# Token factors of an MLP as a row through DRAM, and the order of loads and PSUM banks in its lower stage

## The chip, the cores and the metric

The kernel runs on one core of one Trainium2 chip. The metric is device microseconds of one execution; less is better. One profiled execution comes with instruction times of all engines.

## The reference, cut to what matters

One decoder layer over 1032 tokens (1024 of a prompt and 8 of a sample batch) with 1024 channels: a mixer of attention and retention, a cross-attention into memory tokens, and an MLP, each behind an RMSNorm and with a residual addition. The change lies in the MLP:

```python
def rmsnorm(x, g):
    xf = x.astype(jnp.float32)
    y = xf * lax.rsqrt(jnp.mean(xf * xf, axis=-1, keepdims=True) + EPS)
    return (y * g.astype(jnp.float32)).astype(x.dtype)

def sq_relu_mlp(h, w_up, w_down):
    return jnp.square(jax.nn.relu(h @ w_up)) @ w_down

xp = xp + sq_relu_mlp(rmsnorm(xp, norm_mlp[l]), w_up[l], w_down[l])
```

All is float32. The hidden width is 4096.

## The kernel before, in words

Channels lie on partitions, tokens in columns. A float32 operand is split into a high part (`wh`, `UH`, `T_h`) by an ACT cast and a low part (`wl`, `UL`, `T_l`) by a DVE subtraction, and a product of two operands takes three matmuls: high by high, high by low, low by high. Tokens are handled in four column groups of 258 (`QC`): two halves of 516 tokens by two chunks, `c` = 0 and 1. `QCOLS[2 * c + half]` are the columns.

*Before the MLP* the output projection of the cross-attention runs over `(ft, c)`, channel tile by column group, in a list `order` written out by hand; here `c` runs over the four column groups, and the list ends with (6, 2), (7, 2), (4, 3), (5, 3), (6, 3), (7, 3). Each step evicts its bank by a DVE addition into `xs` (L1716); ACT scales it by the MLP's gain (L1719) and squares it (L1724); POOL adds the squares into `ssum` (L1725); ACT's DMA queue stores `xs` to `X3` in DRAM (L1726).

*Token factors.* `norm_factor(x)` makes the RMSNorm's factor of column group `x`: a matmul with a 128x128 tile of ones sums `ssum` over partitions and repeats the sum on all of them, ACT takes the square root (L1612), DVE the reciprocal (L1613), and the factors stay in `ssum`. They are applied after the upper projection, in `hidden`: DVE computes max(product, 0) times the factor (L1772) and ACT squares it (L1773).

*The upper stage* does the projection to the hidden width with seven products instead of eight in each 2x2 block (a Strassen-Winograd form). There are 16 blocks `b`; `up_block` runs products `q` in the order 1, 6, 2, 7, 5, 4, 3, and inside each the chunks. A product is twelve matmuls of 258 columns (L1747). Banks are called X (q 1 and 2), Z (6, 7 and 4) and Y (5 and 3), two of each; two more banks hold other tiles, the sums of `norm_factor` among them. `p1` is an ACT copy of X (L1794), `u2` and `u3` are Z plus `p1` (L1797, L1802), the quadrants 22, 21, 12 are formed at L1806. When all four quadrants of a chunk are there, ACT's queue stores three of them to `HQ`, and POOL forms four differences `ht` (L1779 to L1782) and stores them to `HT` (L1783). Block 0 runs for chunk 0 alone first, while the operands of chunk 1 are being made (`first_half`, `second_half`), then for chunk 1.

*The lower stage* goes back to 1024 channels, also with seven products, over four groups `g` of hidden rows and, inside each, four pairs `p` of output tiles. For each group, `raw_d` tiles hold the weights of the pairs; `left_lower` casts and splits them into `wd` (L1875, L1876), for product 6 after differences on DVE and POOL (L1885 to L1889). `right_lower` loads hidden operands from `HQ` or `HT` into `raw_h` on SP (L1862) and splits them (L1868, L1869). Products run in stages (1, 2), (6,), (7, 4), (5, 3); stages of two products run pairs 0 and 1 first, then 2 and 3; stage (6,) runs all four pairs. Each product is again twelve matmuls (`dn`, L1897), and its bank is added by DVE into result tiles `C` (L1977), or copied by ACT (L1975) for product 1 of the first group. `residual_rows` loads the residual from `X3` into `C` on SP (L1849). At the end, `finish` makes the final norm's factors with Sqrt and reciprocal and stores.

*What sets the order.* TensorE's instructions in both stages keep the order of the program (`tc.keep_in_program_order`). The instructions of the other engines and of the DMA queues are put in order by the framework's planner, which goes by its own modelled times; each engine and each queue then runs its list strictly in that order. `tc.issue_after(ins)` puts what follows behind `ins` on its queue. A tile waits, when its memory was used before, for the last user of that tile (`reuse_waits="tile"`). In the first group the weights of pair 0 are issued by SP and those of pairs 1 to 3 by POOL:

```python
(nc.gpsimd if g == 0 and p else nc.sync).dma_start(raws[p][x][:, :1024], i["wall"][U_DN + 8 * g + 2 * p + x])
```

The eight lower banks come from one pool tag with eight buffers (`tag="acc", bufs=8`). The first tiles of pairs 2 and 3 (`raw_d0_2_0`, `raw_d0_3_0`) lie in the memory of the last block's `hq` tiles, of chunk 0 and chunk 1.

An existing function, `rstd_bcast` (L1150 to L1165), makes the factors of an earlier norm in another way: sums in one row, an ACT copy (L1159), a DMA that lays the row out as 86 partitions by 12 columns (L1161), multiply-add on DVE and power -0.5 on POOL (`rsqrt_small`, L120 and L121), a DMA to DRAM (L1164) and one that reads the row back to all 128 partitions (L1165).

Of the kernel before, what the change touches and what calls it, by code (L numbers as in the profile page):

```python
# [10 lines left out]
F32 = mybir.dt.float32  # L11
# [8 lines left out]
P = 128  # L20
D = 1024
# [27 lines left out]
def decoder_step(ctx: ExitStack, tc: tile.TileContext, i: dict, o: dict):  # L49
# [1515 lines left out]
    for q, kt, half in ((1, 0, lo_h), (6, 0, hi_h), (2, 4, lo_h), (3, 4, hi_h)):  # L1565
        for c in range(2):
            cq = slice(half.start + c * QC, half.start + c * QC + QC)
            RIGHT[q, c] = [x[:, kt : kt + 4, cq] for x in (UH, UL)]
# [38 lines left out]
    def norm_factor(x):  # L1607
        cs = QCOLS[x]
        fp = PD.tile([P, 512], F32, tag=("mk", "dt")[x % 2], name=f"rm_{x}", bufs=1)[:, :QC]
        mm(fp, onesq, ssum[:, cs], True, True)  # L1610
        rf = ssum[:, cs]
        nc.scalar.activation(rf, fp, AF.Sqrt, scale=1.0 / D, bias=epsc)  # L1612
        nc.vector.reciprocal(rf, rf)  # L1613
# [26 lines left out]
    with pool("e") as A, pool("e_ps", space=PSUM) as PS:  # L1640
# [59 lines left out]
        for n, (ft, c) in enumerate(order):  # L1700
# [36 lines left out]
            if (ft, c) == (5, 3):  # L1737
                parts_st.close()
                right_tiles(1, 5, 7)

# [11 lines left out]

    def up_block(b, W, chunks):

# [9 lines left out]
        def hidden(quad, src, c):  # L1764
            if c not in HQ_:
                if (b, c) == (0, 0):
                    HQ_[c] = N.tile([P, 4, QC], F32, tag="hq0", name="hq_0_0")
                else:
                    HQ_[c] = N.tile([P, 4, QC], F32, tag=f"xq{2 + c}_0", name=f"hq_{b}_{c}")
            h = HQ_[c]  # L1770
            r = small("r", f"{quad}_{c}", 4) if quad == 11 else src
            nc.vector.scalar_tensor_tensor(r, src, 0.0, ssum[:, QCOLS[2 * c + HALF_OF[quad]]], ALU.max, ALU.mult)  # L1772
            nc.scalar.activation(h[:, PLACE[quad], :], r, AF.Square)  # L1773
            if quad == 12:
                nc.scalar.dma_start(HQ[b, c].rearrange("p (x j) -> p x j", x=3), h[:, 0:3, :])

                h11, h21, h22, h12 = (h[:, x, :] for x in range(4))
                t = N.tile([P, 4, QC], F32, tag=f"xq{2 + c}_1", name=f"ht_{b}_{c}")
                nc.gpsimd.tensor_sub(t[:, 0, :], h12, h11)  # L1779
                nc.gpsimd.tensor_sub(t[:, 1, :], h22, t[:, 0, :])  # L1780
                nc.gpsimd.tensor_sub(t[:, 2, :], h22, h12)
                nc.gpsimd.tensor_sub(t[:, 3, :], h21, t[:, 1, :])  # L1782
                nc.gpsimd.dma_start(HT[b, c].rearrange("p (x j) -> p x j", x=4), t)  # L1783

        for q in (1, 6, 2, 7, 5, 4, 3):
            for c in chunks:
# [11 lines left out]
                elif q == 2:  # L1798
                    hidden(11, ps, c)
                elif q == 7:  # L1800
                    u3[c] = small("u3", c)
                    nc.vector.tensor_add(u3[c], ps, p1[c])  # L1802
                else:
                    quad, x = {5: (22, u3), 4: (21, p1), 3: (12, u2)}[q]
                    r = small("r", f"{quad}_{c}", 4)
                    nc.vector.tensor_add(r, ps, x[c])  # L1806
                    hidden(quad, r, c)
# [7 lines left out]
    norm_factor(0)  # L1815
    norm_factor(1)
    with pool("h") as HP, pool("s_ps2", space=PSUM) as SP:
        pin[0] = True
        up_block(0, w0, (0,))
# [4 lines left out]
        norm_factor(2)  # L1824
        norm_factor(3)
# [11 lines left out]
    STAGES = [(1, 2), (6,), (7, 4), (5, 3)]  # L1837
    SOURCE = {1: (HQ, 0), 2: (HQ, 1), 3: (HQ, 2), 5: (HT, 0), 6: (HT, 1), 7: (HT, 2), 4: (HT, 3)}
    taken = [0, 0]
    with pool("acc", side="right") as AC, pool("w") as A, pool("w_ps", space=PSUM) as PS:  # L1840

# [5 lines left out]
        def residual_rows(quad):  # L1847
            kh, hs = {11: (0, lo_h), 21: (4, lo_h), 22: (4, hi_h), 12: (0, hi_h)}[quad]
            nc.sync.dma_start(C[quad], X3[kh : kh + 4, :, hs].rearrange("k p c -> p k c"))  # L1849
# [64 lines left out]
        def finish(c, half):  # L1914
            tail = tails[c] if half else None
            cs = QCOLS[2 * c + half]
            fp = PS.tile([P, 512], F32, tag="acc", name=f"fin_{c}_{half}", bufs=8)[:, :QC]
# [15 lines left out]
        for g in range(4):  # L1933
# [10 lines left out]
            for p, x in ((0, 0), (0, 1), (1, 0), (1, 1), (2, 0), (2, 1), (3, 0), (3, 1)):  # L1944

                (nc.gpsimd if g == 0 and p else nc.sync).dma_start(raws[p][x][:, :1024], i["wall"][U_DN + 8 * g + 2 * p + x])
            for stage in STAGES:
                if (g, stage[0]) == (0, 1):
                    residual_rows(11)
                S = {q: right_lower(g, q) for q in stage}  # L1950
                if (g, stage[0]) == (0, 7):

                    with tc.issue_after(seen["SP"]):
                        for quad in (22, 21, 12):
                            residual_rows(quad)
                end = g == 3 and stage == (5, 3)
                batches = [(0, 1), (2, 3)] if len(stage) == 2 else [(0, 1, 2, 3)]
                if end:
                    batches = [(0, 1, 2, 3)]
                bank = {}  # L1960
                steps = [(q, p, c) for batch in batches for q in stage for p in batch for c in range(2)]
                if end:
                    steps = [(q, p, c) for c in range(2) for q in stage for p in range(4)]
                W = {}
                for n, (q, p, c) in enumerate(steps):
                    if (q, p) not in W:
                        W[q, p] = left_lower(g, p, q)
                    if q == stage[0]:
                        bank[p, c] = PS.tile([P, 512], F32, tag="acc", name=f"dn_{g}_{q}_{p}_{c}", bufs=8)[:, :QC]
                    ps = bank[p, c]  # L1970
                    lower(W[q, p], S[q], c, ps, q == stage[0])
# [212 lines left out]
```

## Time and profile before

| what | value |
|---|---|
| median of three runs | 1566.5 us |
| the three runs | 1566.5, 1566.89, 1562.6 us |
| profiled execution, its time | 1562.22 us |
| its span, first to last instruction | 1560.5 us |
| mean granted TensorE clock | 0.988 |
| PE busy | 1497.6 us (96%) |
| DVE, ACT, POOL busy | 1070.7, 651.0, 442.5 us |
| DMA | 230.02 MB, mean 147 GB/s |

Times in the views are microseconds from the span's start. PE is TensorE's matmuls, PEld its weight loads, DVE VectorE, ACT ScalarE, POOL GpSimd, SP SyncE; a `q` behind an engine's name (SPq) is its DMA-issuing queue. In the timeline a row has start, duration, engine, line, operation, out<-in, and in brackets the engine's idle time before it and what ended it; consecutive instructions of one kind are merged into one row with a count, and their durations overlap. In the waits a row has who waited for whom, then the total in us, the number of times and the longest. A fenced row starts where the profile puts it; releasers are inferred from semaphores. The upper stage starts near 873 us, the lower stage at 1209.8 us.

### The profile page before, as it was taken

What the parts mean: (1) busy time and instruction counts of PE and PEld (TensorE: products, weight loads), DVE (VectorE), ACT (ScalarE), POOL (GpSimd) and SP (SyncE); (2) the same over time, 40 slices, a digit from 0 to 9 for tenths busy, and PEclk for the clock granted to TensorE, in tenths of its full rate; (3) what the DMA queues carried; (4) which work ended last, traced back from release to release, by engine and by line L of the source; (5) the groups of instructions that cost most, each with busy time, mean ns of one, the idle gap of its engine ahead of it and who ended that gap; (6) DMA issues with size and microseconds to landing.
All of it is one profiled execution on the core that took longest, in us unless ns stands there. A gap on an engine that the chain in (4) does not pass through costs nothing.

```text
span 1560.5 us, 26766 instructions
## 1 busy us (share of the span) xinstructions
PE 1497.6 (96%) x10483; PEld 1395.5 (89%) x10483; DVE 1070.7 (69%) x2096; ACT 651.0 (42%) x1265; POOL 442.5 (28%) x457
## 2 busy tenths in 40 slices
PE   9989999999899899999999899999999899999997
PEld 7667868999859789989899899999999799999996
DVE  4224422898875744566686988888788588787887
ACT  6314332665652332036634543333334343334454
POOL 0343311113452520134322233433334402020360
PEclk9999999999999999999999999999999899999998
DMA  8635343313675246462584244434335872636313
GB/s 286 173 92 166 82 112 95 88 38 96 176 272 196 77 163 179 147 188 99 153 275 148 91 147 150 150 136 150 136 137 182 275 231 80 196 85 201 97 42 109
DMA packets 121875, 230.02 MB, mean 147 GB/s; under 512 B 14210, under 2 KB 74481, under 8 KB 121621
## 3 DMA queue, kind: packets, MB, share of 16 engines
q1 hardware_dynamic: 91508, 170.30, 34.9%
q0 software_dynamic: 21024, 41.10, 8.6%
q10 hardware_dynamic: 9216, 16.91, 2.8%
q8 instruction: 82, 1.34, 0.4%
q14 instruction: 45, 0.36, 0.1%
HBM read 168.93 MB, written 57.52 MB: 145 GB/s over the span
## 4 chain that ended last, share of the span: by engine, by line
PE 48%; DVE 12%; DMA 5%; issue 4%; ACT 3%; POOL 1%; DVEq 0%; POOLq 0%; ACTq 0%; SPq 0%
PE dn L1897 17%; PE Z L1747 7%; PE mq L67 5%; PE Y L1747 5%; PE pr_m L67 4%; PE X L1747 4%; PE pr_o L67 3%; DVE wu L1586 1%; DMA raw_up<-in_wall 1%; DVE dacc L1187 1%; PE mpv L67 1%; PE ms L67 1%; DMA raw_d<-in_wall 1%; POOL ck L546 1%; DVE wd L1876 1%
## 5 line engine op out<-in xcount | busy, mean ns | idle before, releaser
L1897 PE MATMUL dn<-UH,wd 128*128 128x258 f32 x1792 | 328.7, 285 | 7.6 <-ACT wd L1875 4.4
L1897 PEld LDWEIGHTS dn<-UH,wd 128*128 128x128 f32 x1792 | 280.4, 191 | 9.3 <-ACT wd L1875 4.9
L1897 PE MATMUL dn<-UL,wd 128*128 128x258 f32 x896 | 254.6, 284 | 0.0
L1897 PEld LDWEIGHTS dn<-UL,wd 128*128 128x128 f32 x896 | 170.9, 191 | 0.1
L1773 ACT ACTIVATE hq<-r 128x258 f32<-128x258 f32 x128 | 53.6, 419 | 161.1 <-DVE r L1772 160.9
L1977 DVE TENSOR_TENSOR c<-c,dn 128x258 f32<-128x258 f32 x216 | 88.2, 417 | 36.9 <-PE dn L1897 34.8
L1747 PE MATMUL Z<-T_h,wu 128*128 128x258 f32 x512 | 100.1, 287 | 6.4 <-DVE u L1797 4.7
L1875 ACT CAST wd<-raw_d 128x512 fp32r<-128x512 f32 x96 | 58.9, 618 | 104.8 <-PE dn L1897 84.7
L1586 DVE TENSOR_TENSOR wu<-raw_up,wu 128x512 fp32r<-128x512 f32 x96 | 91.9, 958 | 9.1 <-ACT wu L1585 9.1
L1747 PE MATMUL X<-UH,wu 128*128 128x258 f32 x512 | 97.7, 283 | 0.4 <-ACT p L1794 0.4
L110 DVE TENSOR_TENSOR wl_u<-raw_u,wh_u 128x1024 fp32r<-128x1024 f32 x46 | 58.4, 1279 | 57.3 <-ACT wh_u L109 55.4
L1747 PEld LDWEIGHTS Z<-T_h,wu 128*128 128x128 f32 x512 | 81.4, 189 | 9.5 <-DVE u L1797 7.1
L1876 DVE TENSOR_TENSOR wd<-raw_d,wd 128x512 fp32r<-128x512 f32 x96 | 75.4, 789 | 18.0 <-ACT wd L1875 17.9
L1747 PEld LDWEIGHTS X<-UH,wu 128*128 128x128 f32 x512 | 81.3, 188 | 0.7 <-ACT p L1794 0.6
L109 ACT CAST wh_u<-raw_u 128x1024 fp32r<-128x1024 f32 x50 | 52.2, 1050 | 70.9 <-PE mq L67 43.6
L1868 ACT CAST UH<-raw_h 128x1032 fp32r<-128x1032 f32 x56 | 58.8, 1055 | 51.6 <-PE dn L1897 30.9
L1779 POOL TENSOR_TENSOR ht<-hq 128x258 f32<-128x258 f32 x32 | 23.4, 730 | 200.8 <-ACT hq L1773 186.8
L1869 DVE TENSOR_TENSOR UL<-raw_h,UH 128x1032 fp32r<-128x1032 f32 x56 | 76.3, 1362 | 5.3 <-ACT UH L1868 5.3
L1889 POOL TENSOR_TENSOR raw_d<-raw_d,raw_d 128x512 f32<-128x512 f32 x16 | 23.4, 1460 | 182.0 <-DVE raw_d L1885 127.6
L1747 PE MATMUL Z<-T_l,wu 128*128 128x258 f32 x256 | 72.4, 283 | 0.0
L1747 PE MATMUL X<-UL,wu 128*128 128x258 f32 x256 | 72.2, 282 | 0.0
L1585 ACT CAST wu<-raw_up 128x512 fp32r<-128x512 f32 x96 | 57.1, 610 | 30.6 <-DVE raw_up L1592 23.7
(483 smaller groups left out, 4630.8 us busy)
## 6 DMA issues: line engine op xcount, KB each, us to landing
raw_u<-in_wall SPq DMA_DIRECT2D x59, 512.0 KB, 4.6
HT<-ht POOLq DMA_DIRECT2D x32, 516.0 KB, 3.0
raw_h<-HT SPq DMA_DIRECT2D x32, 516.0 KB, 4.4
raw_up<-in_wall SPq DMA_DIRECT2D x32, 512.0 KB, 3.6
raw_d<-in_wall SPq DMA_DIRECT2D x26, 512.0 KB, 4.5
HQ<-hq ACTq DMA_DIRECT2D x32, 387.0 KB
raw_h<-HQ SPq DMA_DIRECT2D x24, 516.0 KB, 4.5
cmk<-in_cmk SPq DMA_DIRECT2D x16, 512.0 KB, 4.8
```

Source lines behind the costliest of these rows:

```text
L67: pinned(nc.tensor.matmul(out, l, r, start=start, stop=stop))
L110: (lo_engine or nc.vector).tensor_sub(wl[:, :n], raw[:, :n], wh[:, :n].bitcast(F32))
L1585: nc.scalar.copy(w[:, :512], src)
L1586: nc.vector.tensor_sub(w[:, 512:], src, w[:, :512].bitcast(F32))
L1747: pinned(nc.tensor.matmul(ps, l, r[:, k, :], start=first and k == 0 and x == 0, stop=k == 3 and x == 2, skip_group_check=True))
L1773: nc.scalar.activation(h[:, PLACE[quad], :], r, AF.Square)
L1868: nc.scalar.copy(h, rv)
L1869: nc.vector.tensor_sub(l, rv, h.bitcast(F32))
L1875: nc.scalar.copy(w[:, :512], src)
L1876: nc.vector.tensor_sub(w[:, 512:], src, w[:, :512].bitcast(F32))
L1897: pinned(nc.tensor.matmul(ps, l, r[:, k, cq], start=first and k == 0 and x == 0, stop=k == 3 and x == 2, skip_group_check=True))
L1977: nc.vector.tensor_add(y, y, ps)
```

## The change

- `norm_factor` goes. `norm_rows(c, row_tile)` makes the factors of the two column groups of one chunk: two matmuls against a single column of ones, an ACT copy of each one-partition row, a DMA on ACT's queue into `col` (86 partitions, three columns for each group), multiply-add and power -0.5 on POOL, POOL's DMA to DRAM and two POOL DMAs that read the rows back to all partitions, into `ssum`. It is called for chunk 0 after the projection step (7, 2), and for chunk 1 inside block 0's first run, behind product 2 and ahead of its `hidden`.
- In block 15, chunk 1, the four `ht` differences go from POOL to DVE.
- In the lower stage's first group all weights are issued by SP: pairs 0 and 1 first, pairs 2 and 3 after the operand loads of products 1, 2 and 6; the residual of quadrant 11 is loaded in two halves around product 6's operands; operands of 7 and 4, then the other residuals, are put behind these loads. Its products run as (1, 2) on pairs 0 and 1, 6 on pairs 0 and 1, (1, 2) on pairs 2 and 3, 6 on pairs 2 and 3. The other groups keep their order.
- The eight lower banks get tags `acc0` to `acc7`, placed in this order and taken in turn.

```diff
+    def norm_rows(c, row_tile):
+        for x in (2 * c, 2 * c + 1):
+            cx = slice(3 * x, 3 * x + 3)
+            rp = PD.tile([P, 512], F32, tag=("mk", "dt")[x % 2], name=f"rm_{x}", bufs=1)[:1, :QC]
+            mm(rp, ones, ssum[:, QCOLS[x]], True, True)
+            row = row_tile(x)[:1]
+            nc.scalar.copy(row, rp)
+            nc.scalar.dma_start(col[:, cx], row)
+        cc = slice(6 * c, 6 * c + 6)
+        nc.gpsimd.tensor_scalar(col[:, cc], col[:, cc], 1.0 / D, EPS, ALU.mult, ALU.add)
+        nc.gpsimd.tensor_tensor(col[:, cc], col[:, cc], half[:86, 0:1].to_broadcast([86, 6]), op=ALU.pow)
+        r = rrow[3:4, 2 * c * QC : (2 * c + 2) * QC]
+        nc.gpsimd.dma_start(r.rearrange("a (x p k) -> p (a x) k", x=2, k=3), col[:, cc].rearrange("p (x k) -> p x k", x=2))
+        for x in range(2):
+            nc.gpsimd.dma_start(ssum[:, QCOLS[2 * c + x]], bcast_rows(r[:, x * QC : x * QC + QC], P, QC))
...
+            if (ft, c) == (7, 2):
+                norm_rows(0, lambda x: A.tile([P, QC], F32, tag="xs", name=f"nrow_{x}", bufs=3))
...
+                eng = nc.vector if (b, c) == (15, 1) else nc.gpsimd
...
                 elif q == 2:
+                    if then:
+                        then()
                     hidden(11, ps, c)
...
-    norm_factor(0)
-    norm_factor(1)
...
-        up_block(0, w0, (0,))
+        up_block(0, w0, (0,), lambda: norm_rows(1, lambda x: HP.tile([P, QC], F32, tag="r", name=f"nrow_{x}", bufs=4)))
...
-        norm_factor(2)
-        norm_factor(3)
...
+        turns = [0]
+        for x in BANK_ORDER:
+            PS.tile([P, 512], F32, tag=f"acc{x}", name=f"acc{x}_order", bufs=1)
+        def acc_bank(name):
+            turns[0] += 1
+            return PS.tile([P, 512], F32, tag=f"acc{(turns[0] - 1) % 8}", name=name, bufs=1)[:, :QC]
...
-            for p, x in ((0, 0), (0, 1), (1, 0), (1, 1), (2, 0), (2, 1), (3, 0), (3, 1)):
-                (nc.gpsimd if g == 0 and p else nc.sync).dma_start(raws[p][x][:, :1024], i["wall"][U_DN + 8 * g + 2 * p + x])
+            load_left((0, 1) if g == 0 else range(4))
+            parts = [((1, 2), (1, 2), (0, 1)), ((), (1, 2), (2, 3)), ((6,), (6,), (0, 1)), ((), (6,), (2, 3))]
+            if g == 0:
+                parts = [parts[0], parts[2], parts[1], parts[3]]
+            parts += [((7, 4), (7, 4), (0, 1)), ((), (7, 4), (2, 3)), ((5, 3), (5, 3), (0, 1)), ((), (5, 3), (2, 3))]
+            if g == 3:
+                parts[-2:] = [((5, 3), (5, 3), (0, 1, 2, 3))]
+            for new, qs, ps_ in parts:
+                if g == 0 and 7 in new:
+                    with tc.issue_after(seen["SP"]):
+                        S.update({q: right_lower(g, q) for q in new})
                     with tc.issue_after(seen["SP"]):
                         for quad in (22, 21, 12):
                             residual_rows(quad)
+                else:
+                    S.update({q: right_lower(g, q) for q in new})
+                if g == 0 and 1 in new:
+                    residual_rows(11, (slice(0, 2),))
+                if g == 0 and 6 in new:
+                    residual_rows(11, (slice(2, 4),))
+                    load_left((2, 3))
```

More of the change, by code (lines that the diff above doesn't have):

```diff
@@ L1605, in put @@
         nc.vector.tensor_sub(l, src, h.bitcast(F32))
[L1607 to L1613, printed above, removed]
+    col = KC.tile([86, 12], F32, tag="ncol", name="ncol")
+    def norm_rows(c, row_tile):
[13 more added lines that the diff above has]
+            nc.gpsimd.dma_start(ssum[:, QCOLS[2 * c + x]], bcast_rows(r[:, x * QC : x * QC + QC], P, QC))
     def first_half(c):
@@ L1916, in finish @@
             cs = QCOLS[2 * c + half]
-            fp = PS.tile([P, 512], F32, tag="acc", name=f"fin_{c}_{half}", bufs=8)[:, :QC]
+            fp = acc_bank(f"fin_{c}_{half}")
             mm(fp, onesq, ssf[:, cs], True, tail is None)
@@ L1955, in decoder_step @@
                             residual_rows(quad)
-                end = g == 3 and stage == (5, 3)
-                batches = [(0, 1), (2, 3)] if len(stage) == 2 else [(0, 1, 2, 3)]
-                if end:
[L1959 to L1964, printed above, removed]
+                else:
[5 more added lines that the diff above has]
+                    load_left((2, 3))
+                end = g == 3 and 5 in qs
+                steps = [(q, p, c) for q in qs for p in ps_ for c in range(2)]
+                if end:
+                    steps = [(q, p, c) for c in range(2) for q in qs for p in ps_]
                 for n, (q, p, c) in enumerate(steps):
@@ L1967, in decoder_step @@
                         W[q, p] = left_lower(g, p, q)
-                    if q == stage[0]:
-                        bank[p, c] = PS.tile([P, 512], F32, tag="acc", name=f"dn_{g}_{q}_{p}_{c}", bufs=8)[:, :QC]
+                    if q == qs[0]:
+                        bank[p, c] = acc_bank(f"dn_{g}_{q}_{p}_{c}")
                     ps = bank[p, c]
-                    lower(W[q, p], S[q], c, ps, q == stage[0])
+                    lower(W[q, p], S[q], c, ps, q == qs[0])
                     cq = slice(c * QC, c * QC + QC)
```

32 lines of the change are left out of this document (17 added, 15 removed).

## The prediction

> **What bounds the kernel now.** I read the page's busy times first, then the windows of TensorE, then the waits and the timeline at the two places that the change touches.
>
> ```profile
> PE 1497.6 (96%) x10483; PEld 1395.5 (89%) x10483; DVE 1070.7 (69%) x2096; ACT 651.0 (42%) x1265; POOL 442.5 (28%) x457
> ```
>
> TensorE is the bound: it is busy for 1497.6 of 1560.5 us, and the change takes no product away. Time can only come from what TensorE loses between products: gaps, and stretches at a lower clock. The windows show where it loses (stretch, its length, PE busy, matmuls, granted clock, DMA share, GB/s):
>
> ```profile
> core 0: us, PE busy (x), PEclk, DMA share, GB/s
> 872.80:892.40 19.60, 17.18 (x131) 1.00 0.38 115
> 892.40:895.00 2.60, 0.69 (x6) 1.00 0.51 199
> 1209.80:1250.00 40.20, 33.22 (x233) 0.87 0.79 268
> 1300.00:1400.00 100.00, 100.00 (x838) 1.00 0.47 138
> 1214.60:1218.00 3.40, 3.40 (x19) 0.51 0.71 239
> 1229.50:1235.40 5.90, 5.78 (x25) 0.52 1.03 412
> ```
>
> Undisturbed, 838 matmuls take 100 us: 0.119 us each, 1.43 us for a product of twelve. In the first 40.2 us of the lower stage stand 233 matmuls, worth 233 x 0.1193 = 27.8 us. So 12.4 us are lost there: 40.2 - 33.2 = 7.0 us idle, and 5.4 us in the two stretches at half clock. The waits of 860 to 910 us (first three rows, the start of the upper stage) and of 1195 to 1260 us (the start of the lower stage) name what ended the gaps:
>
> ```profile
> PE Z L1747 <- DVE u L1797: 2.8, 2, 1.9
> PE Z L1747 <- DVE xs L1716: 1.1, 1, 1.1
> PE X L1747 <- ACT p L1794: 0.4, 1, 0.4
> ...
> PE dn L1897 <- ACT wd L1875: 4.4, 1, 4.4
> PE dn L1897 <- DVE r L1806: 1.8, 1, 1.8
> PE dn L1897 <- DVE wd L1876: 0.6, 1, 0.6
> ```
>
> That is 4.3 us at the first place and 6.8 us at the second. Everything the change can win lies here, some 17 us with the slow clock.
>
> **Part 1: the token factors.** Out go four Sqrt on ACT, four reciprocals on DVE and the Sqrt table's load at this place. The timeline around them:
>
> ```profile
> 875.41 1.28 ACT L1612 ACT_TABLE_LOAD   x1
> ...
> 877.45 3.37 DVE L1613 RECIPROCAL ssum<-ssum 128x258 f32<-128x258 f32 x2
> ...
> 878.15 0.37 ACT L1794 COPY p<-X 128x258 f32<-128x258 f32 x1
> ...
> 880.75 0.35 DVE L1797 TENSOR_TENSOR u<-Z,p 128x258 f32<-128x258 f32 x1
> ...
> 887.07 1.03 PE L67 MATMUL rm<-ssum,onesq 128*128 128x258 f32 x4
> ...
> 892.23 1.75 DVE L1613 RECIPROCAL ssum<-ssum 128x258 f32<-128x258 f32 x1
> ```
>
> The copy `p`, for which TensorE waited 0.4 us, stands behind the table load and two Sqrt. The first `u`, released at 880.75, stands behind two reciprocals that end at 880.8; the second, longest wait (1.9 us) stands behind the reciprocal of 892.23. With them gone 0.4 + 2.8 = 3.2 us go. The 1.1 us for `xs` stay: the bank is released by a DVE addition that is queued behind operand splits, not behind factors. The sums over partitions remain four matmul groups at the same 258 columns, only earlier on the queue: 0.
>
> What comes in is a chain: sum, ACT row copy, ACT's DMA into `col`, two POOL operations, POOL's DMA to DRAM, POOL's DMA that reads the row back to all partitions. The kernel does the same for its second norm, once for the whole row, on the SP queue:
>
> ```profile
> 578.94 0.72 SPq L1161 DMA_DIRECT2D rcol<-rrow  x1
> 581.00 0.17 DVE L120 TENSOR_SCALAR rcol<-rcol 86x12 f32<-86x12 f32 x1 [2.12 <-DMA rcol<-rrow]
> 581.25 2.27 POOL L121 TENSOR_TENSOR rrc<-rcol,half 86x12 f32<-86x12 f32 x1 [6.63 <-DVE rcol L120]
> 583.55 0.25 SPq L1164 DMA_DIRECT2D rrow<-rrc  x1
> 585.23 0.33 SPq L1165 DMA_DIRECT2D rb<-rrow  x1
> ...
> 588.83 0.94 DVE L1329 SCALAR_TENSOR_TENSOR qm<-mq,rb 128x344 f32<-128x344 f32 x2 [7.66 <-DMA rb<-rrow]
> ...
> L121 POOL TENSOR_TENSOR rm<-sm,half x1: 708/708/708, 599.8 to 599.8; 128x2 f32<-128x2 f32 x1
> ...
> HT<-ht POOLq DMA_DIRECT2D x32, 516.0 KB, 3.0
> ```
>
> From these rows: DMA into the column 2.1 us (578.94 to 581.00), power between 0.7 us (2 columns) and 2.3 us (12 columns), so 1.3 us for 6, the write 1.7 us (583.55 to 585.23), or 3.0 us if it goes like POOL's own stores, the read back 3.6 us (585.23 to 588.83). With 0.8 us for two row copies and at most 0.7 us for the POOL multiply-add, a chain takes 10.2 to 11.5 us. In a sentence by itself: the Trainium skill, page "DMA: Bandwidth & Descriptors", section "Anatomy of one DMA", gives each DMA issued by POOL about 2.0 us of fixed time, nearly all of it the receipt of the write, by which three in a row would be an estimated 6 to 7 us; the rows' 7.4 us are what I use.
>
> Is that hidden? The first pair's chain starts after the product (7,2), four projection products (24 matmuls, 2.86 us each) before the upper stage, and its factor is first used after three products of that stage: 11.4 + 4.3 = 15.7 us against 11.5. Yes, with 4 us in hand. The second pair's chain starts behind the block's third product. Today that pair's sums start at 887.07, behind four more products (5.7 us) and a wait for `u` of 0.9 us (2.8 - 1.9), so the third product ends at 880.5, and without the 0.4 us at 880.1. The sums add 0.8 us: the chain starts at 880.9 and lands at 891.1 to 892.4. The first user is the DVE multiplication of the second chunk's `hidden(11)`, after seven more products: 880.9 + 7 x 1.43 = 890.9. So DVE stands waiting up to 1.5 us; behind it are queued `u3`, operand splits and, through `u3`, TensorE's product 4, two products later at 893.8. With 0.8 us for the two DVE operations the row may land as late as 893.0 before TensorE waits. I take 0, with 3 us as the far end, as if both POOL DMAs took 1.5 us more than these rows. POOL itself holds nothing: its next work, `ht` of block 0, starts after 892. ACT gets four issues of 0.3 us for two Sqrt pairs. The table load is not saved but moves to the first final factor, where ACT has room (row of 1530, below): 0.
>
> **Part 2: the start of the lower stage.** The rows of the two large waits:
>
> ```profile
> 1212.83 0.42 DVE L1806 TENSOR_TENSOR r<-Y,u 128x258 f32<-128x258 f32 x1
> ...
> 1213.30 0.39 PE L1897 MATMUL dn<-UH,wd 128*128 128x258 f32 x1 [1.83 <-DVE r L1806]
> 1213.46 0.75 POOL L1779 TENSOR_TENSOR ht<-hq 128x258 f32<-128x258 f32 x1 [11.62 <-ACT hq L1773]
> ...
> 1220.79 0.56 POOL L1946 DMA_DIRECT2D raw_d<-in_wall  x1
> ...
> 1228.86 0.62 ACT L1875 CAST wd<-raw_d 128x512 fp32r<-128x512 f32 x1 [9.08 <-DMA raw_d<-in_wall]
> ...
> 1229.53 0.58 PE L1897 MATMUL dn<-UH,wd 128*128 128x258 f32 x1 [4.39 <-ACT wd L1875]
> ...
> raw_d<-in_wall SPq DMA_DIRECT2D x26, 512.0 KB, 4.5
> ...
> raw_d<-in_wall POOLq DMA_DIRECT2D x6, 512.0 KB, 9.4
> ```
>
> Banks: the second product already waits for the upper stage's last reader of a Y bank, while X and Z banks have long been read. Taking the banks as 0 to 7, in the order in which the upper stage gives them back, puts the Y banks at products 7 and 8, 10 us later: 1.8 us go.
>
> Loads: the weights of pairs 2 and 3 are issued by POOL at 1220.79, behind its eight `ht` subtractions (1213.46 on), and land 8 us later. In the change half of the subtractions go to DVE, so their source tiles come free after four of 0.73 us: 1213.46 + 2.9 = 1216.4. SP issues the loads there, ahead of the residual rows with which they shared the engines. Besides, the product 6 of pairs 0 and 1 goes in between, so pair 2 is due not after 8 but after 12 products, at 1209.8 + 17.2 = 1227, less 1.3 us for cast and split: 1225.7. At 4.5 to 8 us of landing it is there at 1221 to 1224.5; pair 3, 1 MB behind at the 412 GB/s of the window of 1229.5, comes 2.5 us later, 1223.5 to 1227, and is due at 1228.5. The 4.4 us go; I keep 1 us for pair 3 and for the small wait of 0.6 us, which nothing here removes.
>
> What the SP queue now holds up behind these loads, the operands of products 7 and 4 and three residual rows, is needed from 24 products on, 1209.8 + 34.4 = 1244, over 20 us after the loads are issued: 0. The four subtractions on DVE are 4 x 0.42 = 1.7 us, in a stretch where it is busy for 6.4 of 10 us (columns: PE, PEld, DVE, ACT, POOL):
>
> ```profile
> 1210.00:1220.00 10.00, 8.17 (x56) 7.97 (x55) 6.40 (x10) 5.13 (x12) 6.52 (x8) 0.83 0.89 276
> ...
> 1530.00:1540.00 10.00, 8.32 (x67) 8.01 (x66) 9.70 (x16) 4.44 (x12) 0.00 (x0) 1.00 0.57 192
> ```
>
> Clock: both half-clock stretches begin within a few microseconds of a gap, 1214.6 after the 1.8 us and 1229.5 after the 4.4 us. Without the gaps I let all 5.4 us go. The Trainium skill, "TensorE: Matmul & The Clock Gate", Part 1, says that the clock halves only after an idle window of about 3.4 us; by that the first stretch, after 1.8 us of idleness, would have another cause and stay. The trace disagrees at least in part: its 1.8 us gap is followed by clock 0.51, though the 1.9 us gap at 892.4 is followed by 1.00.
>
> **The sum.** First place 3.2; second place 1.8 + 4.4 + 5.4 - 1.0 = 10.6; together 13.8 us. The profiled execution took 1562.2 us (span 1560.5 and 1.7 around it) and would come to 1548.4. The median of the three runs, 1566.5, lies 4.3 us above it, the lowest at 1562.6; from the median it is 1552.7. I say 1553.
>
> **The rivals.**
> *The row comes late.* DVE's queue stands before `hidden(11)` and TensorE waits as it did for the reciprocals. For: the second chain has 2 us to spare at most (893.0 - 891.1), and two of its DMAs are on POOL. Against: the same chain took 9.9 us in this trace. It costs up to 3 us: 1556.
> *The loads stay late.* SP issues in order; if pair 2's tile is free only at about 1221, because POOL's or DVE's subtractions still end then, landing at 8 us gives 1229, and 2 to 3 us of gap with a clock stretch of 2.8 us remain. Against: the tile needs four subtractions, not eight. It leaves 7 to 8 us of gain: 1559.
> *The first slow stretch stays*, since the clock follows something else than the 1.8 us gap: 3.4 - 19 x 0.119 = 1.1 us less: 1554.
> *The upper stage's DVE order gets worse (slower).* Only TensorE's order is pinned; the others' order comes from a planner, and an edit at its start can move `u` behind an operand split in every one of the 16 blocks, as it stood behind `reciprocal` here. Price: about 0.9 us (2.8 - 1.9) per such wait. One per block, 14 us, makes it even; two per block, 29 us, ends at 1582. Against: in the whole trace, with the same planner, TensorE waits for `u` six times:
>
> ```profile
> PE Z L1747 <- DVE u L1797: 4.7, 4, 1.9
> ...
> PE Z L1747 <- DVE u L1802: 1.5, 2, 1.1
> ```
>
> **How the numbers follow.** Forecast 0.58, row late 0.15, loads late 0.13, slow stretch 0.06, upper stage worse 0.08. What a measurement of this kernel can tell from no change is about 0.3%, 4.7 us, so faster means under 1561.8. The first four cases end between 1548 and 1559 on the median's scale, and up to 4 us lower on the profiled one's; a late row and late loads together could reach 1562. Faster 0.82; same 0.10 (both late, or a few upper blocks worse); slower 0.08. Range 1546 to 1562: the low end is 1548.4 with the kept 1 us and the 1.1 us of `xs` gone too, the high end both late cases together.
>
> **What would show it.** In the changed profile: no reciprocal and no table load near 875; waits on `u` at the start of the upper stage gone, those on `xs` still there; the DVE factor multiplication of chunk 1 waiting on the DMA of the row for at most 2 us; the second `dn` product directly behind the first; `raw_d` of pairs 2 and 3 issued by SP near 1216 (less what was won before); clock 1.00 through the first 40 us of the lower stage with about 330 matmuls in them. Wrong would be: a PE wait on `r` or `u` behind the row's DMA, a wait on `wd` of over 2 us, or new DVE waits spread over the upper blocks.

## The result, and the profile after

| kernel | median us | ratio to before, 95% interval | upper stage | lower stage |
|---|---|---|---|---|
| before | 1565.0 (20 executions) | | 336.3 | 339.0 |
| changed | 1571.9 (20 executions) | 1.0044 [1.0029, 1.0058] | 345.5 | 336.7 |

The change made the kernel slower by 0.44%, where 1553 us had been forecast. The last two columns are from the profiled executions: from the first upper product to the first lower one, and from there to the start of the last lower matmul. The upper stage lost 9.2 us and the lower one gained 2.3; together 6.9 us, the difference of the medians. The profiled spans differ by 10.6 us (1571.1 against 1560.5); the other 3.7 us had been lost ahead of the first upper product (877.3 against 873.6 us), 3.4 of them already at the start of the projection ahead of it (775.0 against 771.6 us), up to which the change edits nothing. In the profiles of all thirteen kernels of this document that projection starts between 770.9 and 777.5 us, so this part says nothing of the change.

The waits of TensorE in the changed kernel, at the start of the upper stage and at the start of the lower one (total us, times, longest):

```profile
PE Z L1760 <- DVE u L1818: 8.0, 2, 6.4
PE X L1760 <- ACT p L1808: 2.8, 1, 2.8
PE Z L1760 <- DVE xs L1727: 0.2, 1, 0.2
...
PE dn L1919 <- ACT c L2011: 4.3, 1, 4.3
PE dn L1919 <- DVE c L2013: 1.7, 1, 1.7
```

At the first place 4.3 us have become 11.0. At the second the waits for `r` and `wd` are gone, and two for result tiles `c` have come. The windows (PE busy, matmuls, granted clock, DMA share, GB/s) show that the clock fell behind the longest waits too:

```profile
870.00:890.00 20.00, 16.98 (x122) 0.91 0.35 93
890.00:910.00 20.00, 11.98 (x94) 0.93 0.46 103
910.00:930.00 20.00, 20.00 (x154) 0.90 0.41 136
1222.70:1262.90 40.20, 35.94 (x279) 0.92 0.69 240
1250.00:1255.00 5.00, 4.36 (x20) 0.50 0.53 139
```

Where the upper stage's time went is read on POOL. Its timeline in the changed kernel (start, duration, idle time before and what ended it in brackets):

```profile
870.37 0.92 POOL L1619 TENSOR_SCALAR ncol<-ncol 86x6 f32<-86x6 f32 x1 [2.86 <-DMA ncol<-nrow]
871.37 2.19 POOL L1620 TENSOR_TENSOR ncol<-ncol,half 86x6 f32<-86x6 f32 x1
873.85 1.75 POOL L1622 DMA_DIRECT2D rrow<-ncol  x1 [0.30 <-POOL ncol L1620]
875.63 0.66 POOL L1736 TENSOR_TENSOR ssum<-ssum,sqc_m 128x258 f32<-128x258 f32 x1
880.37 1.15 POOL L1624 DMA_DIRECT2D ssum<-rrow  x2 [4.08 <-DMA rrow<-ncol]
881.53 2.09 POOL L1736 TENSOR_TENSOR ssum<-ssum,sqc_m 128x258 f32<-128x258 f32 x3
895.18 0.86 POOL L1619 TENSOR_SCALAR ncol<-ncol 86x6 f32<-86x6 f32 x1 [11.55 <-DMA ncol<-nrow]
896.12 1.36 POOL L1620 TENSOR_TENSOR ncol<-ncol,half 86x6 f32<-86x6 f32 x1
897.77 1.67 POOL L1622 DMA_DIRECT2D rrow<-ncol  x1 [0.30 <-POOL ncol L1620]
902.96 1.11 POOL L1624 DMA_DIRECT2D ssum<-rrow  x2 [3.52 <-PE Y L1760]
```

The first chain's write is issued at 873.85, and the read behind it only at 880.37: 6.5 us. Behind that read stand three square sums of the projection's last steps, which run at 881.53. ACT has two square tiles and waits for them; DVE waits for the second chain's factors:

```profile
882.22 0.42 ACT L1735 ACTIVATE sqc_m<-xs 128x258 f32<-128x258 f32 x1 [2.73 <-POOL ssum L1736]
...
883.12 0.37 ACT L1808 COPY p<-X 128x258 f32<-128x258 f32 x1
...
889.21 0.36 ACT L1616 COPY nrow<-rm 1x258 f32<-1x258 f32 x1
...
907.01 0.43 DVE L1785 SCALAR_TENSOR_TENSOR r<-X,ssum 128x258 f32<-128x258 f32 x1 [6.96 <-issue]
```

For the last row the profile names no releaser; that it waits for the factors is inferred from its operand `ssum`, which the chain's last DMA writes. ACT's 2.73 us become TensorE's 2.8 us for `p`, and the second chain's row copy starts at 889.21, 11.9 us into the stage instead of the predicted 7.3 (880.9 - 873.6). From there to the factors at 907.01 pass 17.8 us.

### The profile page after: what moved, and what is told of

It reads as the page before. It is cut to its first block, busy times and chain, and to the rows that moved or that the text cites. A ratio compares the mean times of both kernels' runs of the same rounds, so it can differ in the third digit from the quotient of the medians.

```text
span 1571.1 us, 26799 instructions
## 1 busy us (share of the span) xinstructions
PE 1502.7 (96%) x10483; PEld 1397.9 (89%) x10483; DVE 1066.5 (68%) x2096; ACT 652.7 (42%) x1265; POOL 449.8 (29%) x457
## 4 chain that ended last, share of the span: by engine, by line
PE 50%; DVE 11%; DMA 5%; issue 4%; ACT 2%; POOL 1%; DVEq 0%; ACTq 0%; POOLq 0%; SPq 0%
PE dn L1919 16%; PE Z L1760 8%; PE Y L1760 5%; PE mq L67 5%; PE X L1760 5%; PE pr_m L67 4%; PE pr_o L67 3%; PE mpv L67 1%; DVE dacc L1187 1%; PE mv L67 1%; DMA raw_h<-HT 1%; PE mk L67 1%; PE ms L67 1%; DMA raw_up<-in_wall 1%; DVE wu L1586 1%
```

## The experiments

Theory one, *hold*: POOL, waiting for the write, holds the square sums, through them ACT, and so the start of the second chain. Theory two, *long chain*: the chain is half as long again as predicted, wherever it starts. A third question is which part of the lower stage's edits brought its gain, and where the rest of the forecast 10.6 us went. Ratios are to the kernel before on the same chip.

| kernel | ratio, 95% interval | upper | lower |
|---|---|---|---|
| lower stage alone | 0.9974 [0.9957, 0.9991] | 335.7 | 336.9 |
| rows alone | 1.0053 [1.0034, 1.0073] | 345.0 | 339.2 |
| rows' write and reads by SP | 1.0003 [0.9985, 1.0022] | 335.4 | 338.2 |
| sums on DVE | 1.0006 [0.9990, 1.0022] | 338.2 | 339.8 |
| copies first | 0.9965 [0.9949, 0.9980] | 337.9 | 332.8 |
| old product order | 0.9968 [0.9951, 0.9985] | 335.3 | 333.7 |
| banks alone | 0.9995 [0.9978, 1.0012] | 336.2 | 339.4 |
| rows on SP, 24 bytes | 0.9968 [0.9949, 0.9986] | 332.6 | 335.9 |
| rows on POOL, 24 bytes | 0.9990 [0.9969, 1.0011] | 334.8 | 336.1 |
| both repairs | 0.9938 [0.9914, 0.9961] | 332.5 | 333.8 |
| both, old product order | 0.9947 [0.9921, 0.9972] | 332.7 | 332.6 |

A stage is good to about 2 us: the same lower stage took 335.9 to 339.8 us in six of these profiles, the same upper stage 335.3 to 337.9 in five. The old lower stage took 339.0 to 339.4 us in three (before, rows alone, banks alone).

**The lower stage alone** (the changed kernel with `norm_factor` put back):

```diff
-            if (ft, c) == (7, 2):
-                norm_rows(0, ...)
+    norm_factor(0)
+    norm_factor(1)
...
-        up_block(0, w0, (0,), lambda: norm_rows(1, ...))
+        up_block(0, w0, (0,))
...
+        norm_factor(2)
+        norm_factor(3)
```

> The changed lower stage alone; the token factors as before (Sqrt and reciprocal). My theory is that all of the loss comes from the row and that the lower stage brought a little: upper stage (first upper product to first product of the lower stage) back from 345.4 to about 336 us, lower stage at 337 us against 339.4, so a time about 2 us under the kernel before (ratio 0.997 to 1.000). Rival: the lower stage loses too, through its new wait of 4.3 us for ACT's copies of product 1, and gained in the profile only by chance: ratio 1.001 to 1.003.

It is faster than before by 0.26%. The first theory of this run holds: all of the loss comes from the rows, and the wait for ACT's copies (3.7 us here) only eats part of the gain.

**The rows alone** (the kernel before with `norm_rows` in place of `norm_factor`, at the same two calls):

> The row of token factors alone; the lower stage as before. If the row is the whole loss: upper stage 345 us against 336, TensorE waiting for u about 8 us and for the copy p about 3 us near its start, ratio 1.005 to 1.007, and the ratios of this kernel and of the lower stage alone add up to that of the whole change (1.0044). If instead the two parts disturb each other, this one is near 1.000.

The upper stage takes 345.0 us, TensorE waits 7.0 us for `u` and 2.8 for `p` (the profile is of the slowest of six executions). The two parts alone make 1.0053 - 0.0026 = 1.0027, a little under the whole change's 1.0044, with intervals that overlap; nothing asks for a disturbance between them.

**The rows' write and reads by SP** (the column still by ACT, the pieces as in the change):

```diff
-        nc.gpsimd.dma_start(r.rearrange(...), col...)
+        nc.sync.dma_start(r.rearrange(...), col...)
         for x in range(2):
-            nc.gpsimd.dma_start(ssum[:, QCOLS[2 * c + x]], bcast_rows(...))
+            nc.sync.dma_start(ssum[:, QCOLS[2 * c + x]], bcast_rows(...))
```

> The whole change, but the write of the row and its two reads back are issued by SP and not by POOL, so that POOL waits for neither. Theory POOL holds: the square sums of the projection's last steps, which stood on POOL behind the wait for the row's write, run at once; ACT is not held, the 2.8 us of TensorE for the copy p go, the second chain starts about 3 us earlier, and the wait of 6.4 us for u shrinks to about 3; upper stage near 339 us, ratio to the kernel before about 1.000. Theory long chain: the chain from the row copy to the factors takes 17 to 18 us whoever issues the DMAs; the 2.8 us go, but 6 us for u stay, upper stage near 342 us, ratio 1.002 to 1.003. If SP's write takes the 1.7 us that the earlier norm's row showed and not POOL's 5 to 6, the chain falls to 13 us and both waits go.

The wait for `p` is gone, the one for `u` is 3.0 us in all, and the upper stage is back at 335.4 us, better than either theory had it and nearest to the expectation's last case. The SP queue of this run:

```profile
870.08 0.26 SPq L1622 DMA_DIRECT2D rrow<-ncol  x1
872.98 0.83 SPq L1624 DMA_DIRECT2D ssum<-rrow  x2
...
886.27 0.26 SPq L1622 DMA_DIRECT2D rrow<-ncol  x1
889.58 1.79 SPq L1624 DMA_DIRECT2D ssum<-rrow  x2
```

The writes take 2.9 and 3.3 us, and the second chain 14.0 (881.05 to 895.06). Open: its ratio is 0.3% above that of the lower stage alone, though the profiled stages hardly differ; the profiled execution (1560.6 us) is the fastest of this kernel's twelve, median 1565.8, so its stages may not be typical.

**The square sums on DVE** (the chain untouched, with nothing queued behind POOL's wait):

```diff
-                nc.gpsimd.tensor_add(ssum[:, cs], ssum[:, cs], sq)
+                (nc.vector if n >= 22 + 6 else nc.gpsimd).tensor_add(ssum[:, cs], ssum[:, cs], sq)
```

> The whole change, but the square sums of the projection's last four steps are added by DVE and not by POOL, where they stood behind the wait for the row's write. The chain itself is untouched. Theory POOL holds: ACT is no longer held by the square tiles, so the copy p is in time (2.8 us go) and the second chain's row copies start about 2 to 3 us earlier, with the wait for u down from 6.4 to about 3.5; upper stage about 340 us, ratio about 1.001. Theory long chain: only the 2.8 us go, u keeps its 6 us: upper stage 342.5 us, ratio 1.0025. Four additions of 0.4 us on DVE, in a stretch where operand splits queue, could cost up to 1.7 us.

TensorE's waits at the start of the upper stage, and POOL's rows of the second chain:

```profile
PE Z L1760 <- DVE u L1818: 6.4, 2, 5.4
```

```profile
883.66 0.20 POOL L1619 TENSOR_SCALAR ncol<-ncol 86x6 f32<-86x6 f32 x1 [4.90 <-DMA ncol<-nrow]
883.94 1.87 POOL L1620 TENSOR_TENSOR ncol<-ncol,half 86x6 f32<-86x6 f32 x1
886.11 1.67 POOL L1622 DMA_DIRECT2D rrow<-ncol  x1 [0.29 <-POOL ncol L1620]
894.37 1.11 POOL L1624 DMA_DIRECT2D ssum<-rrow  x2 [6.59 <-DMA rrow<-ncol]
```

This tells the two theories apart. The wait for `p` is gone: that one was the hold. The chain now starts at 880.5, 6.3 us into the stage where the prediction had 7.3, and ends at 898.0: still 17.5 us, though made up differently (column 3.1 us instead of 6.0, write 8.3 instead of 5.2). TensorE waits 5.4 us at once for `u`: that one is the long chain. The upper stage falls from 345.5 to 338.2 us, lower than either theory had it, and the ratio from 1.0044 to 1.0006.

**Copies first** (the lower stage alone, with ACT's casts of product 6 for pairs 2 and 3 queued behind its copies of product 1):

```diff
                     if (q, p) not in W:
-                        W[q, p] = left_lower(g, p, q)
+                        if g == 0 and q == 6 and p >= 2:
+                            with tc.issue_after(seen["ACT"]):
+                                W[q, p] = left_lower(g, p, q)
+                        else:
+                            W[q, p] = left_lower(g, p, q)
...
                     if g == 0 and q == 1:
                         nc.scalar.copy(y, ps)
+                        seen["ACT"] = nc.cur_bb.bb.instructions[-1]
```

> The changed lower stage with the old token factors, and in its first group ACT's casts of product 6's weights for pairs 2 and 3 queued behind ACT's copies of product 1 on these pairs. In the lower stage alone TensorE waited 3.7 us for those copies, which stood on ACT behind casts that DVE released late. Theory queue order: the 3.7 us and the half clock behind them (about 2 us) go, lower stage about 332 us instead of 337, ratio to the kernel before 0.994. Rival: DVE is the bound there and the casts, now later, make TensorE wait for the weights of product 6 instead: lower stage unchanged at 337 us, ratio 0.997.

Why the copies were late is seen on ACT in the changed kernel:

```profile
1248.65 0.62 ACT L1897 CAST wd<-s 128x512 fp32r<-128x512 f32 x1 [2.68 <-DVE s L1908]
1249.18 1.14 ACT L1897 CAST wd<-raw_d 128x512 fp32r<-128x512 f32 x2
1250.22 0.64 ACT L2011 COPY c<-dn 128x258 f32<-128x258 f32 x2
```

Product 2 adds to the bank of product 1, so TensorE stands from 1246.4 to 1250.6 us until ACT has copied product 1 out; the copy stands behind a cast that waits for DVE, which works for a product that comes later. With the copies first the waits of the stage's start are these:

```profile
PE dn L1910 <- ACT c L2006: 1.8, 1, 1.8
...
PE dn L1910 <- DVE wd L1889: 1.4, 1, 1.4
PE dn L1910 <- DVE c L2009: 1.4, 1, 1.4
```

The lower stage falls to 332.8 us with the clock at 1.00, as queue order would have it. The waits add up to 4.6 us instead of the 6.5 of the lower stage alone (3.7 for ACT's copies, 2.8 for a result tile), so about half of the 4.1 us gained is left for the clock, which was 0.91 over two stretches of 20 us there. The ratio, 0.9965, lies nearer to the rival's 0.997, and against 0.9974 it puts the gain at 0.1%, with intervals that overlap: by the times alone this repair is not shown. The upper stage of this profile is 2 us longer than that of the lower stage alone, with the same code: the same gap of 1.9 us was followed here by a clock of 0.89 and 0.77 (895 to 905 us), there by 1.00.

**The old product order** (the lower stage alone; products 1 and 2 on all pairs, then 6; pairs 2 and 3 loaded by SP, in the program right behind the first operands):

```diff
-            if g == 0:
-                parts = [parts[0], parts[2], parts[1], parts[3]]
...
-                    residual_rows(11, (slice(0, 2),))
-                if g == 0 and 6 in new:
-                    residual_rows(11, (slice(2, 4),))
+                    residual_rows(11, (slice(0, 2), slice(2, 4)))
                     load_left((2, 3))
```

> The changed lower stage with the old token factors, but the products of the first group in the order of before: 1 and 2 on all pairs, then product 6; loads in the new order (pairs 2 and 3 by SP, now ahead of product 6's operands), banks in the new order. Theory: the reordering of products is what hides the loads, so without it TensorE waits 2 to 4 us for the weights of pair 2 or 3, and no longer for ACT's copies: lower stage 337 to 339 us, ratio 0.997 to 0.999. Rival: the new order of loads would have been enough, and the reordering only brought the wait for the copies: lower stage 332 to 333 us, ratio 0.994.

The weights, due four products sooner, cost 0.9 and 0.4 us of waits, not 2 to 4, the copies 2.7 us, and the stage took 333.7 us. So the reordering of products was not needed to hide the loads; the other edits were enough, the loads on SP and the four differences on DVE, which no run tells apart. The loads were not ahead of product 6's operands, as the expectation had it: SP issued four operand loads from `HT` first (from 1202.7 us) and the weights at 1213.2 us, 3.6 us into the stage. Nor did the wait for the copies go, which both sides had expected.

**The banks alone** (the kernel before with `acc_bank`):

> The kernel before with the new order of the eight lower banks and nothing else. As the prediction counted it: the wait of 1.8 us for DVE r goes and, with it, the first stretch of half clock (1.6 us): ratio 0.998. Rival: the next wait, for weights that landed at 1228.8 us, 19 us into the stage, does not move, so that TensorE only comes to it sooner: that wait grows from 4.4 to 6 us or more, ratio 1.000.

```profile
PE dn L1905 <- ACT wd L1883: 9.0, 2, 8.2
```

The rival holds. The wait for `r` is gone, and the one for the weights has grown from 4.4 to 8.2 us. ACT could start on these weights 19.4 us into the stage, 19.0 before: TensorE only came sooner to what was late anyway.

**The rows on SP in pieces of 24 bytes** (all of the row's DMAs, and a column of 43 partitions by 6 for each group in place of 86 by 3):

```diff
-            nc.scalar.dma_start(col[:, cx], row)
+            y = 43 * (x - 2 * c)
+            nc.sync.dma_start(col[y : y + 43, 6 * c : 6 * c + 6], row)
...
-        nc.gpsimd.dma_start(r.rearrange("a (x p k) -> p (a x) k", x=2, k=3), col[:, cc].rearrange("p (x k) -> p x k", x=2))
+        nc.sync.dma_start(r.rearrange("a (p k) -> p (a k)", k=6), col[:, cc])
         for x in range(2):
-            nc.gpsimd.dma_start(ssum[:, QCOLS[2 * c + x]], bcast_rows(r[:, x * QC : x * QC + QC], P, QC))
+            nc.sync.dma_start(ssum[:, QCOLS[2 * c + x]], bcast_rows(r[:, x * QC : x * QC + QC], P, QC))
```

> The whole change with the row's transfers all on SP (the two into the column too) and the column laid out so that the write goes in 86 pieces of 24 bytes and not 172 of 12. With SP and 12 bytes the write took 2.9 and 3.3 us and the second chain 14.0 us. If the number of pieces sets the write's time, it falls to about 2 us, the chain to about 12, the wait for u from 2.5 us to under 1, upper stage about 333 us against 335.4, ratio 0.998 to 0.999. If it is latency, the write stays at 3 us, and ratio and upper stage stay at 1.000 and 335 us.

```profile
872.13 0.27 SPq L1622 DMA_DIRECT2D rrow<-ncol  x1
873.81 0.82 SPq L1624 DMA_DIRECT2D ssum<-rrow  x2
...
890.41 0.26 SPq L1622 DMA_DIRECT2D rrow<-ncol  x1
892.96 0.84 SPq L1624 DMA_DIRECT2D ssum<-rrow  x2
```

The writes fall to 1.7 and 2.6 us, the chain to 12.9 (884.65 to 897.54), the waits for `u` to 1.6 us and the upper stage to 332.6 us, under that of the kernel before. Against SP with 12 bytes two things changed, the layout and the column's queue; in the second chain the write became 0.8 us shorter, the column 0.5 and the read back 0.9, and POOL's two operations 1.1 longer. With this the whole change is faster than before.

**The rows on POOL in pieces of 24 bytes** (the layout alone, each DMA on the queue on which the change has it):

> The whole change, transfers on the queues on which it has them (column by ACT, write and reads by POOL), but the write in 86 pieces of 24 bytes instead of 172 of 12. In the whole change the write took 6.5 and 5.2 us from its issue on POOL to the reads; on SP 2.9 and 3.3 us with 12 bytes, 1.7 and 2.6 us with 24. If the pieces are the cost on POOL too, it falls to 3 or 4 us, and with it POOL's hold and the chain: waits for p and u together from 10.8 us to about 5, ratio 1.000 to 1.001. If POOL's queue is the cost whatever the pieces, the write stays over 5 us, TensorE waits about 10 us, ratio 1.004.

```profile
870.21 0.69 POOL L1622 DMA_DIRECT2D rrow<-ncol  x1 [0.30 <-POOL ncol L1620]
...
872.56 1.13 POOL L1624 DMA_DIRECT2D ssum<-rrow  x2 [0.99 <-PE pr_m L67]
...
888.71 0.62 POOL L1622 DMA_DIRECT2D rrow<-ncol  x1 [0.30 <-POOL ncol L1620]
892.42 1.09 POOL L1624 DMA_DIRECT2D ssum<-rrow  x2 [3.09 <-PE X L1760]
```

Half the pieces, on the same queue: the issue takes 0.6 to 0.7 us instead of 1.7, the write 2.4 and 3.7 us instead of 6.5 and 5.2, the wait for `p` is gone and the upper stage takes 334.8 us instead of 345.5. So the many pieces on POOL made the hold and lengthened the write. The second chain falls from 17.8 us to 14.4: 1.5 us in the write, 1.8 in the column, 0.8 in the read back, while POOL's two operations took 0.6 longer. The column's share is not shown to come from its pieces: with 12 bytes on ACT it took 3.1 and 3.6 us in the two runs without the hold above (sums on DVE; write and reads by SP), against 5.9 and 6.0 in the two with it, and 4.2 with 24 bytes here. Either step is enough to undo the loss, larger pieces here or SP with 12 bytes above, though neither kernel is shown to be faster than before; both together gave 2 us more in the profiles.

**Both repairs together**, with the change's product order and with the old one (there all casts of product 6 behind the copies):

> The two repairs together: the row's transfers on SP with pieces of 24 bytes, and ACT's casts for product 6 of pairs 2 and 3 behind the copies of product 1. If the gains of both stages add up: upper stage 333 us, lower stage 333 us against 336 and 339 of before, 9 us less, ratio 0.993 to 0.995. If what one stage wins is lost elsewhere (clock, or a new wait behind it), it stays at the 0.997 of each repair alone.

> The row on SP with pieces of 24 bytes, and the lower stage with the product order of before, the new loads and banks, and all casts of product 6 in the first group behind the copies of product 1. With the old product order alone the lower stage took 333.7 us, with waits of 2.7 us for the copies and 1.3 for weights. If queue order was all of those 2.7 us: lower stage 331 us, ratio 0.993. If the casts come late for product 6 then: lower stage 334 us or more, ratio 0.995.

The gains add up: 0.9938, with a median of 1554.2 us against 1562.7 of before, and 0.9947 with the old product order, which are the same within their intervals. In the first the waits left at the start of the lower stage are 1.4 us at most. Both beat the kernel before and the change.

## Why the prediction was wrong

*The place was right, the sign was not.* The time did lie at the two stage starts, the clock there too, and the sum's second half pointed the right way. The first half failed.

*The length of the row's chain is the first step that failed.* It was put at 10.2 to 11.5 us from the rows of the earlier norm and took 17.8, above all in two terms, the DMA into the column and the write. From one POOL or ACT start to the next:

| step | predicted | changed kernel, second chain |
|---|---|---|
| copies and DMA into the column | 2.9 | 6.0 (889.21 to 895.18) |
| multiply-add, power | 2.0 | 2.6 (to 897.77) |
| write | 1.7 to 3.0 | 5.2 (to 902.96; the first chain's 6.5) |
| read back | 3.6 | 4.1 (to 907.01) |

The write's bounds came from the earlier norm's on SP, which moves twice the data in 86 pieces of 48 bytes (12 columns of a partition), and from POOL's large stores; the new one has 172 pieces of 12. The access pattern stood in the diff, and the prediction looked at queue and bytes, not at pieces. With 12 bytes on SP the write took 2.9 and 3.3 us, with 24 bytes on POOL 2.4 and 3.7, inside or near the predicted bounds; only POOL with 12 bytes lies far outside. The column's 3.1 us above its forecast are the larger term in this chain. ACT made the first DMA's issue (0.63 us) between the two row copies, which explains some 0.7 of them; the rest lies between the second issue at 890.66 and POOL's start at 895.18, and its cause stays open. In the runs without the hold this step took 3.1 to 4.2 us.

The sentence of the Trainium skill that the prediction gave beside its sum ("DMA: Bandwidth & Descriptors", "Anatomy of one DMA": about 2.0 us for each DMA that POOL issues) came no nearer: POOL issues two of the three steps, and they took 5.2 and 4.1 us here, and the formula has no term for pieces; the same page's section "Why small descriptors are slow (HBM only)" names a fixed cost of each packet and each descriptor, which points the way that these runs went, without a price that would give 6.5 us for 172 of them.

*"POOL itself holds nothing" is the second.* The prediction looked for POOL's next work behind the second chain (`ht`), not for the square sums that were queued behind the first one's reads. This cost the 2.8 us for `p` and moved the second chain's start from 7.3 to 11.9 us into the stage. With the sums on DVE the start was 6.3 us into the stage and the wait for `p` gone. That run weighs the two steps: the hold made 7.3 of the 9.2 us by which the upper stage became longer (345.5 to 338.2, before 336.3), and the long chain that was left ate the forecast gain and 1.9 us more.

*The rival "the row comes late" was the right one, at a price far too low.* It was given 3 us at most, as if a late row could cost no more than the two POOL DMAs' 1.5 us each. TensorE waited 8.0 us for `u`, where the forecast had 0; with the hold's 2.8 us and the 0.2 for `xs` that is 6.7 us more than before and, with the clock behind the waits, 9.2. The gain of 3.2 us in this part is real: with the rows on SP in 24-byte pieces the upper stage won 3.7.

*The lower stage.* Its forecast of 10.6 us came out as 2.3 in the profile, and in the medians of the stage alone as 0.26%, some 4 us. The step on the loads was right (SP issued them from 4.4 us into the stage, where the forecast had 6.6, and no wait for `raw_d` is left), though for half of its reason: the product order was not needed. The first slow stretch went too, against the rival that kept it: the clock is 1.00 over the first 20 us. The bank order's 1.8 us were counted by themselves, and the bank order by itself won nothing. In the first 40.2 us stand 279 matmuls, worth 33.3 us: 6.9 us are lost there instead of 12.4. Of this lead of 5.5 us, 1.7 went in the wait for the result tile `c` at 1271.9 us and 1.0 in the wait for the final norm's sums near the end (2.7 us instead of 1.7); the cause of these two is open. What was missing is a queue that the change altered: product 1's bank must be copied before product 2 may add to it, and the planner put that copy behind casts for product 6. (With the old product order 2.7 us of this wait were left, so the reordering is not its only cause; which other edit brings it is open.) This wait of 4.3 us and its half clock (0.50 from 1250 to 1255) took the place of the one removed. No rival named it. Put right, the stage gained 5 to 6 us (332.6 to 333.8 us in four kernels, that of the old product order among them), half of the forecast.

*The slower rival* (worse DVE order in every upper block) did not happen: TensorE waits for `u` at the end of the stage as before, 1.5 us, and once in between, 1.3 us (before 1.9 in two waits). The kernel came out slower for other reasons than the one that this chance of 0.08 stood for.

## What to carry to other kernels

Cost a small DMA by the number and size of its contiguous pieces, read from both access patterns, and only then by its bytes and its queue; a layout that doubles the piece can be worth as much as a better queue. When an engine issues a DMA and then another that must wait for the first, everything behind it on that engine waits too: look for what the same engine still owes to the stage before. When products or loads are reordered, go through each engine's queue for evictions that a later product of the same bank needs, and pin them ahead of casts that are due later.

## What was not expected of the hardware

The write's issue alone kept POOL 1.67 to 1.75 us with 172 pieces and 0.62 to 0.69 us with 86; on SP it was 0.26 us with either. From issue to the reads behind it the same 2 KB took 4.9 to 8.3 us on POOL with 172 pieces, over six writes in three kernels. The traces' semaphore events show why they differ so much: each write reports in 16 parts; with 172 pieces the first part came 3.6 to 3.8 us after the issue in all six, the last 4.3 to 7.7 us after it. With 86 pieces the sixteen came within 0.4 us of each other (1.6 to 1.8 us after the issue in the first write, 2.8 to 3.2 in the second). So with half the pieces the first part came 0.8 to 2.2 us sooner; the rest of the longest writes is late parts, for which no cause is shown.

The clock's fall behind a gap doesn't follow the gap's length alone. A gap of 2.2 us, with shorter ones ahead of it, was followed by 0.66 (old product order, first row), one of 3.0 us by 1.00 (rows on SP in 24 bytes, the other two), and in that same kernel one of 3.2 us by 0.75 again (1260 to 1265 us). The gap of 1.9 us in the upper stage, with the same code, was followed by 0.77 in one kernel and by 1.00 in another (copies first; the lower stage alone). This is one source of the 2 us by which equal stages differ:

```profile
1235.00:1240.00 5.00, 4.59 (x25) 0.66 0.33 120
```

```profile
1235.00:1240.00 5.00, 3.01 (x25) 1.00 0.40 109
1240.00:1245.00 5.00, 5.00 (x44) 1.00 0.90 303
```

The Trainium skill, "TensorE: Matmul & The Clock Gate", Part 1, has the clock decided in windows of about 3.4 us that run freely, not from the gap's start. That a gap of 3.0 us may pass unpunished agrees with it; the falls behind 2.2 us here and 1.8 us in the kernel before do not, if such a window must be idle throughout.
